# Memory squares in other buffers, later first loads of x, and another order for ACT in the second weight block of a two-layer encoder

## The chip, the cores and the metric

The kernel runs on one core of a Trainium2 chip, in one launch. The metric is the device time of one execution in microseconds (us). The engines are PE (TensorE, with PEld for its weight loads), DVE (VectorE), ACT (ScalarE), POOL (GpSimd) and SP (SyncE, which here only issues transfers). Transfers are issued by three queues: SP's and ACT's, and POOL's, which the profile names q1, q10 and q0.

## The reference

A two-layer encoder over 256 tokens `x` of width 2048, with 256 memory tokens `mem` of the same width. In each layer

```
h = rmsnorm(x) ; P = h @ w_in[l]            # 2048 x 7168, split among three mixers
A: short gated convolution (768 columns)
D: differential attention, 6 heads of 128 (two softmaxes of 64-wide halves, ALiBi)
M: cross-attention into the memory, 4 heads of 128:
   mkv = rmsnorm(mem, mem_norm_g[l]) @ w_mem_kv[l]      # 2048 x (512 keys + 512 values)
   mk  = rmsnorm(keys per head) * mem_k_norm_g[l]
x = x + concat(A, D, M) @ w_out[l]
```

All in float32. Only the memory part, `mem` to keys and values of both layers, and the loading of `x` are touched by the change.

## The kernel before, in words

**Products.** Every product is done in three matmuls of a reduced-precision format: an operand is split into a high half `hi` and a low half `lo`, and hi*hi, hi*lo and lo*hi are summed in a bank of PSUM (L312 to L314). `block` (L295) does one such product of 256 tokens with 512 columns of weights. It goes through the 16 row tiles of the weights in 8 chunks of two. For each chunk `load_w` (L274) has SP load 512 KB into `raw` (4 buffers), ACT makes `hi` from it (L290, scaled by the norm's gains; L286 without), DVE makes `lo` (L291, L287), each with 4 buffers, and PE does 12 matmuls of 128x512. So a chunk's weights can be made only when PE has done with the chunk four before, and loaded only when DVE has done with the one four before.

**Order of the work.** The program starts with four memory blocks: keys of layer 0, values of layer 0, keys of layer 1, values of layer 1 (the loop at L764). Then come the blocks of layer 0 on `x`, its output, and the same for layer 1. The `before` hook of `block` is called ahead of each chunk's load: `mem_piece` in the first block, `mem_norm` in the second, `x_load` in the third, `x_squares` in the fourth.

- `mem_piece` (L687) has SP load a piece of `mem` into `xs`, a tile that later holds x. PE turns it, a 128x128 tile at a time, into `pt` (L638, `rows_T`), and ACT and DVE split it into `memT` (L255, L256). In its calls for the sixth and the last chunk it calls `mem_squares` for the first two quarters.
- `mem_squares(c)` (L697) lets ACT square a quarter of the memory's columns, one instruction for each 128 tokens, to sum them into `ssm`. The squares themselves are written to a scratch tile of tag `nat` (3 buffers), where nobody reads them.
- After the first block ACT copies its two banks into `kraw` (L777). Then `mem_norm` (L704) calls `mem_squares(2)` ahead of the second block's first chunk and `mem_squares(3)` ahead of its second, starts `mem_slowly` (the norm's reciprocal root, spread out on DVE, then layer 0's keys) at its third, and loads small constants.
- `x_turned` (L642) brings a strip of x, 512 columns of all tokens, into a tile `xt` of tag `e` (2 buffers) with four transfers, POOL's in layer 0 (L648); five chunks later DVE transposes it (L652) and ACT and DVE split it into `xT`. Its four strips are put on the list at every second chunk of the second block; the first is due four chunks later, so that in the program's text it comes behind all the memory squares. Since the transfer needs nothing but a free buffer, the first two are issued at the program's start.
- `x_load` (L751) loads x a second time, in natural layout, into `xs` when PE has done with `mem`, and calls `rest_of_constants` (L142), a row of small DVE operations on the parameter vectors `vb` and `lam_in`.

**What sets the order on an engine.** The program's text, re-ordered by a scheduler that runs a timeline of its own; instructions marked `keep_in_program_order` keep their order among themselves on an engine. In the first two blocks all of ACT's and DVE's work on weights and `memT` is so marked (`in_order`, L245, `pinned`). Pieces of work that run beside the blocks are generators in `tasks`: `later(g, n)` (L200) makes one due n chunks on, and `run_side` (L217) runs what is due after each chunk. SP's queue is in order: a transfer that waits for its buffer holds back those behind it.

**Tags.** Tiles of one tag share its buffers in turn. `e` (2 buffers) holds the strips `xt` and later attention scores; `nat` (3) holds scratch, among it `lam_in`, squares and `th`; `ga` (1) holds `kraw`, then layer 1's key sheet (L780), then a gate of layer 0; `mqT` (1) holds the query sheet of layer 0 and later other things.

Of the kernel before, what the change touches and what calls it, by code (L numbers as in the profile page):

```python
# [10 lines left out]
F32 = mybir.dt.float32  # L11
# [18 lines left out]
HALF = 64  # L30
MH = W_MEM // P
EPS = 1e-6
NB = 512
# [14 lines left out]
def encoder(ctx: ExitStack, tc: tile.TileContext, x, mem, norm_g, w_in, conv_w, conv_b,  # L48
            dq_g, dk_g, lq1, lk1, lq2, lk2, head_g, mem_norm_g, w_mem_kv, mq_g, mk_g, w_out, out):
    nc = tc.nc  # L50
    x, mem, out = x[0], mem[0], out[0]

    def pool(name, bufs, space=None):
        kw = {"space": space} if space is not None else {}
        return ctx.enter_context(tc.tile_pool(name=name, bufs=bufs, **kw))
# [5 lines left out]
    tmp = pool("tmp", 2)  # L61
# [8 lines left out]
    def nm(s):  # L70
        uid[0] += 1
        return f"{s}_{uid[0]}"
# [13 lines left out]
    lam_in = tmp.tile([P, 4, DEPTH * HALF], F32, tag="nat", name="lam_in", bufs=3)  # L86
# [45 lines left out]
    def g_mnorm(l, k):  # L132
        return cva[:, l * KT + k:l * KT + k + 1]

    cvb = const.tile([P, 64], F32, name="cvb")
    hgain = const.tile([P, DEPTH], F32, name="hgain")
    kgain = const.tile([P, DEPTH], F32, name="kgain")
    mgain = const.tile([P, DEPTH], F32, name="mgain")
    neglam = const.tile([P, DEPTH], F32, name="neglam")
    lam_init = [0.8 - 0.6 * math.exp(-0.3 * l) for l in range(DEPTH)]  # L140

    def rest_of_constants():  # L142
        pb = ps_t.tile([P, NB], F32, tag="t", name="pvb")
        nc.tensor.transpose(pb[:, 0:64], vb, ident[0:64, 0:64])
        nc.vector.tensor_copy(cvb, pb[:, 0:64])
        for l in range(DEPTH):
            nc.vector.tensor_scalar(hgain[:, l:l + 1], cvb[:, 52 + l:53 + l], 1.0 - lam_init[l], None, ALU.mult)
        nc.vector.scalar_tensor_tensor(kgain, cvb[:, 48:48 + DEPTH], HALF ** -0.5, cvb[:, 50:50 + DEPTH],
                                       ALU.mult, ALU.mult)
        nc.vector.tensor_tensor(mgain, cvb[:, 54:54 + DEPTH], cvb[:, 56:56 + DEPTH], ALU.mult)  # L150
        pr = tmp.tile([P, 2, DEPTH, HALF], F32, tag="nat", name="lampr", bufs=3)
        for j in range(2):
            nc.vector.tensor_tensor(pr[:, j].rearrange("p l d -> p (l d)"), lam_in[:, 2 * j], lam_in[:, 2 * j + 1], ALU.mult)
        dots = small.tile([P, 2, DEPTH], F32, tag="dots", name="dots", bufs=1)
        nc.vector.tensor_reduce(dots, pr, AX.X, ALU.add)
        nc.scalar.activation(dots, dots, AF.Exp)
        nc.vector.tensor_tensor(neglam, dots[:, 1], dots[:, 0], ALU.subtract)
        for l in range(DEPTH):
            nc.vector.tensor_scalar(neglam[:, l:l + 1], neglam[:, l:l + 1], -lam_init[l], None, ALU.add)

    slopes = [2.0 ** (-8.0 * (h + 1) / DH) for h in range(DH)]


    class Steps:

# [4 lines left out]
        def __getattr__(self, op):  # L170
            return lambda *a, **k: self.ops.append((op, a, k))
# [24 lines left out]
    side, tasks = deque(), []  # L196
# [3 lines left out]
    def later(g, n):  # L200
        due[id(g)] = chunk[0] + n
        return g
# [192 lines left out]
    def normed(acc, gs, st, home):  # L395
        return normed_steps(nc.vector, acc, gs, st, home)
# [300 lines left out]
    def mem_squares(c):  # L697

        for t in range(NT):
            sq = tmp.tile([P, NB], F32, tag="nat", name=nm("sq"), bufs=3)  # L700
            tc.keep_in_program_order(
                nc.scalar.activation(sq, xs[:, t, c * NB:(c + 1) * NB], AF.Square, accum_out=ssm[:, t, c:c + 1]))  # L702
# [33 lines left out]
    def keys(l, nat):  # L736


        d = dram.tile([NA, B, NA, W_MEM // P * NT * B], F32, name=nm("kd"))
        flat = nat.rearrange("p b j t c -> p b (j t c)")  # L740
        for a in range(NA):
            tc.keep_in_program_order(nc.gpsimd.dma_start(d[:, :, a].rearrange("b c r -> c b r"), flat[a * B:(a + 1) * B]))
        tc.keep_in_program_order(nc.gpsimd.dma_start(flat, d.rearrange("b c a r -> (b c) a r")))
        yield 8
        tc.keep_in_program_order(nc.vector.transpose(
            mkT[l].rearrange("p j (t a i) -> p (j t) a i", t=NT, a=NA),
            nat.rearrange("p a j t c -> p (j t) a c")))
        yield
        tc.keep_in_program_order(nc.scalar.activation(mkT[l], mkT[l], AF.Copy, scale=mgain[:, l:l + 1]))
# [13 lines left out]
    mkT, mv, stm, away, acc_v = [], [], [], [], []  # L763
    for l in range(DEPTH):  # L764
        if l == 0:
            xT = T_tile("xT")
        mkT.append(keep.tile([P, MH, SEQ], F32, tag=f"mkT{l}", name=f"mkT{l}"))

        mv.append(keep.tile([P, NT, W_MEM], F32, tag="mv" if l == 0 else "bgx", name=f"mv{l}"))
        gm = lambda k: g_mnorm(l, k)  # L770
        pinned[0] = l == 0
        acc_k = block(memT, w_mem_kv[l], [(0, NB)], ALLK, gain=gm, before=mem_piece if l == 0 else x_load)
        if l == 0:

            kraw = keep.tile([P, NT, NB], F32, tag="ga", name="kraw")
            for t in range(NT):
                nc.scalar.copy(kraw[:, t], acc_k[t])  # L777
            stm.append(keep.tile([P, 6, NT], F32, tag="stm", name="stm"))
        if l > 0:
            tasks.append(later(keys(l, normed(acc_k, P, stm[0], sheets("ga"))), 10))  # L780
        acc = block(memT, w_mem_kv[l], [(W_MEM, NB)], ALLK, gain=gm, before=mem_norm if l == 0 else x_squares)
        pinned[0] = False
        acc_v.append(acc)
        if l > 0:
            for t in range(NT):
                nc.scalar.activation(mv[l][:, t, :], acc[t], AF.Copy, scale=col(stm[0], R, t))
            away.append(dram.tile([P, NT, W_MEM], F32, name=nm("mvd")))
            nc.sync.dma_start(away[-1], mv[l])
    for l in range(DEPTH):
# [18 lines left out]
        for b in order:  # L808
# [27 lines left out]
        mqT = keep.tile([P, MH, SEQ], F32, tag="mqT", name=nm("mqT"))  # L836
# [147 lines left out]
```

## Time and profile before

| | us |
|---|---|
| time, median of 3 runs | 936.94 (936.02 to 937.57) |
| the profiled execution's own time | 937.88 |
| its span, first to last instruction | 935.3 |
| PE busy | 921.1 |
| DVE busy | 671.3 |
| ACT busy | 499.2 |
| POOL busy | 16.2 |

The mean granted clock of PE over the span is 0.996 of full speed. The profile is of one execution; its page and the views made from its trace give times in us from the span's start, `L286` is a line of the kernel, and `acc<-hi,memT` names what an instruction writes and reads, buffer numbers left out. "xT<-xf" is thus one of the instructions that make x's transposed halves. In a timeline row stand start, duration, engine, line, operation, tiles, shapes and count, and in brackets the idle time ahead of it on its engine with what ended it. Of transfers the profile shows the issue on an engine's queue (SPq), and the packets by queue. Some matmul records can be missing from a trace, a few per cent.

In the page's costliest groups the pattern of the whole run can be seen: a weight chunk costs ACT 1052 ns (L286, 128x1024) or two times 716 (L290, 128x512), DVE 1222 or two times 745 ns, and PE 12 matmuls of about 390 ns each by the record, which overlap.

### The profile page before, as it was taken

The page shows a single profiled execution, that of the slowest core. Times are in us where ns is not written, and L with a number is a line of the kernel's source. Part 1 is how long each engine was busy: PE and PEld are TensorE (multiplying, and loading weights), DVE is VectorE, ACT ScalarE, POOL GpSimd, SP SyncE. Part 2 cuts the span into 40 slices and gives each one's busy share as a digit, 9 for nine tenths or more (in the row PEclk, how much of TensorE's full clock was granted, in tenths as well). Part 3 has the DMA queues.
Part 4 walks back from the last instruction along what each step waited for, and adds up shares of the span by engine and source line. Part 5 has one row for each costly group of instructions (what it writes and reads, how often), then busy time and mean ns, then how long its engine had stood idle before and what let it go on. Part 6 is the DMA issues. An engine that isn't in the chain of part 4 may idle for free.

```text
span 935.3 us, 12301 instructions
## 1 busy us (share of the span) xinstructions
PE 921.1 (98%) x4170; PEld 762.7 (82%) x4170; DVE 671.3 (72%) x1206; ACT 499.2 (53%) x779; POOL 16.2 (2%) x34
## 2 busy tenths in 40 slices
PE   6899999999999999999999999999999999999998
PEld 4688888888888888888888888888888888888886
DVE  3589977867789786566776757887898776558652
ACT  4666844576545554445555554568654454436431
POOL 2002100000000000000000000000000000000000
PEclk9999999999999999999999999999999999999999
DMA  9599778885678999989587766886889979988662
GB/s 249 172 297 267 247 266 230 244 237 171 195 211 219 240 269 248 237 271 248 205 256 263 243 198 201 235 246 185 241 226 222 257 215 252 250 243 235 215 216 78
DMA packets 251138, 215.05 MB, mean 230 GB/s; under 512 B 131182, under 2 KB 174020, under 8 KB 251076
## 3 DMA queue, kind: packets, MB, share of 16 engines
q1 hardware_dynamic: 248292, 208.76, 76.5%
q0 software_dynamic: 1440, 4.20, 1.8%
q10 hardware_dynamic: 1344, 1.33, 0.5%
q8 instruction: 32, 0.52, 0.2%
q14 instruction: 30, 0.25, 0.1%
HBM read 193.26 MB, written 20.97 MB: 229 GB/s over the span
## 4 chain that ended last, share of the span: by engine, by line
PE 98%; DMA 1%; ACT 0%; SPq 0%; issue 0%; DVE 0%; DVEq 0%
PE acc L313 31%; PE acc L312 31%; PE acc L314 31%; PE po L462 2%; DMA xs<-in_mem_dram 1%; PE s L615 1%; PE s L570 1%; PE s L569 1%; PE pt L638 0%; SPq L691 0%; ACT kraw L777 0%; SPq L280 0%; ACT sq L702 0%; ACT hi L290 0%; DVE xs L945 0%
## 5 line engine op out<-in xcount | busy, mean ns | idle before, releaser
L286 ACT CAST hi<-raw 128x1024 fp32r<-128x1024 f32 x288 | 302.8, 1052 | 349.7 <-PE acc L314 284.4
L287 DVE TENSOR_TENSOR lo<-raw,hi 128x1024 fp32r<-128x1024 f32 x288 | 351.7, 1222 | 188.3 <-ACT hi L286 184.9
L312 PE MATMUL acc<-hi,xT 128*128 128x512 f32 x896 | 350.5, 392 | 0.0
L314 PE MATMUL acc<-hi,xT 128*128 128x512 f32 x896 | 349.0, 390 | 0.0
L313 PE MATMUL acc<-lo,xT 128*128 128x512 f32 x896 | 348.9, 389 | 0.0
L314 PEld LDWEIGHTS acc<-hi,xT 128*128 128x128 f32 x896 | 168.2, 188 | 35.0
L313 PEld LDWEIGHTS acc<-lo,xT 128*128 128x128 f32 x896 | 168.3, 188 | 34.1
L312 PEld LDWEIGHTS acc<-hi,xT 128*128 128x128 f32 x896 | 168.2, 188 | 34.0
L312 PE MATMUL acc<-hi,yT 128*128 128x512 f32 x256 | 99.6, 389 | 0.0
L314 PE MATMUL acc<-hi,yT 128*128 128x512 f32 x256 | 99.6, 389 | 0.0
L313 PE MATMUL acc<-lo,yT 128*128 128x512 f32 x256 | 99.6, 389 | 0.0
L313 PEld LDWEIGHTS acc<-lo,yT 128*128 128x128 f32 x256 | 48.1, 188 | 10.1
L312 PEld LDWEIGHTS acc<-hi,yT 128*128 128x128 f32 x256 | 48.1, 188 | 10.1
L314 PEld LDWEIGHTS acc<-hi,yT 128*128 128x128 f32 x256 | 48.1, 188 | 9.8
L291 DVE SCALAR_TENSOR_TENSOR lo<-raw,cva,hi 128x512 fp32r<-128x512 f32 x64 | 45.8, 745 | 13.6 <-ACT hi L290 13.2
L290 ACT ACTIVATE hi<-raw,cva 128x512 fp32r<-128x512 f32 x64 | 42.6, 716 | 16.7 <-DMA raw<-in_w_mem_kv_dram 15.4
L313 PE MATMUL acc<-lo,memT 128*128 128x512 f32 x124 | 49.9, 403 | 0.0
L314 PE MATMUL acc<-hi,memT 128*128 128x512 f32 x124 | 49.3, 398 | 0.0
L312 PE MATMUL acc<-hi,memT 128*128 128x512 f32 x124 | 46.0, 404 | 2.5 <-ACT hi L290 2.5
L312 PEld LDWEIGHTS acc<-hi,memT 128*128 128x128 f32 x124 | 23.5, 194 | 7.8 <-ACT hi L290 3.0
L313 PEld LDWEIGHTS acc<-lo,memT 128*128 128x128 f32 x124 | 24.0, 193 | 6.0 <-DVE lo L291 0.9
L314 PEld LDWEIGHTS acc<-hi,memT 128*128 128x128 f32 x124 | 24.0, 194 | 4.9
(156 smaller groups left out, 643.0 us busy)
## 6 DMA issues: line engine op xcount, KB each, us to landing
raw<-in_w_in_dram SPq DMA_DIRECT2D x192, 512.0 KB, 4.4
raw<-in_w_out_dram SPq DMA_DIRECT2D x64, 512.0 KB, 4.1
raw<-in_w_in_dram SPq DMA_DIRECT2D x64, 256.0 KB, 4.3
raw<-in_w_mem_kv_dram SPq DMA_DIRECT2D x31, 512.0 KB, 6.2
d<-sh SPq DMA_DIRECT2D x80, 128.0 KB, 3.6
sh<-d SPq DMA_DIRECT2D x64, 128.0 KB, 4.5
d<-yn SPq DMA_DIRECT2D x40, 64.0 KB, 3.9
yn<-d SPq DMA_DIRECT2D x40, 64.0 KB, 4.4
```

Source lines behind the costliest of these rows:

```text
L286: nc.scalar.copy(hi, raw)
L287: nc.vector.tensor_tensor(lo_, raw, hi.bitcast(F32), ALU.subtract)
L290: in_order(nc.scalar.activation(hi[:, j], raw[:, j], AF.Copy, scale=gains_of(j)), nc.vector.scalar_tensor_tensor(lo_[:, j], raw[:, j], gai ...
L291: nc.vector.scalar_tensor_tensor(lo_[:, j], raw[:, j], gains_of(j), hi[:, j].bitcast(F32), ALU.mult, ALU.subtract))
L312: nc.tensor.matmul(acc[t], sh, hi, start=first, stop=False)
L313: nc.tensor.matmul(acc[t], sh, lo, start=False, stop=False)
L314: nc.tensor.matmul(acc[t], sl, hi, start=False, stop=last)
L462: nc.tensor.matmul(po[:, t, :], eT[:, i, t, k, :], v[:, k, h * P:(h + 1) * P], start=k == 0, stop=k == NT - 1)
L569: nc.tensor.matmul(s[c][:, i, :], qi, k_first(yT, c, h), start=True, stop=False)
L570: nc.tensor.matmul(s[c][:, i, :], qi, k_second(yT, k2, c, h), start=False, stop=True)
L615: nc.tensor.matmul(s[:, i, :], qT[:, h, i * P:(i + 1) * P], kT[:, h, :], start=True, stop=True)
```

## The change

Four things are done.

1. `mem_squares` writes its scratch to tag `e` instead of `nat`. The tag's two buffers are those of the strips of x, and all eight squares come ahead of the first strip in the program's text.
2. In the second block `mem_norm` calls `mem_squares(2)` ahead of the second chunk (k of 2) instead of the first, copies the first block's banks to `kraw` ahead of the third (k of 4) instead of right after the first block, calls `mem_squares(3)` ahead of the fourth (6 instead of 2), and starts `mem_slowly` at the fifth (8 instead of 4). The copies are now kept in program order.
3. The operations of `rest_of_constants` on DVE are kept in program order, by a wrapper `InOrder`.
4. Layer 1's key sheet takes tag `mqT` instead of `ga`.

In the built program the order on the queues and engines changes as follows. POOL issues the first eight transfers of strips behind a wait for ACT, four for each strip. ACT makes the second block's first weights right after the first block's last, then squares a quarter, makes the second weights, copies the two banks, makes the third, squares the last quarter, and goes on with weights. On PE the transposes of the fourth piece of mem (two row tiles each; the first piece is loaded in two parts) stand ahead of the first full chunk's matmuls, not among them. On SP the four loads of `lam_in` stand among the weights of the first block instead of behind four loads of the second. On DVE the first operations of `rest_of_constants` (L145 to L150) stand in the third block instead of the first, and `mem_slowly` runs two chunks later.

```diff
     def rest_of_constants():
+        vec = InOrder()
         pb = ps_t.tile([P, NB], F32, tag="t", name="pvb")
         nc.tensor.transpose(pb[:, 0:64], vb, ident[0:64, 0:64])
-        nc.vector.tensor_copy(cvb, pb[:, 0:64])
+        vec.tensor_copy(cvb, pb[:, 0:64])
...
+    class InOrder:
+
+
+        def __getattr__(self, op):
+            return lambda *a, **k: tc.keep_in_program_order(getattr(nc.vector, op)(*a, **k))
...
     def mem_squares(c):
 
         for t in range(NT):
-            sq = tmp.tile([P, NB], F32, tag="nat", name=nm("sq"), bufs=3)
+
+            sq = tmp.tile([P, NB], F32, tag="e", name=nm("msq"))
             tc.keep_in_program_order(
                 nc.scalar.activation(sq, xs[:, t, c * NB:(c + 1) * NB], AF.Square, accum_out=ssm[:, t, c:c + 1]))
 
     def mem_norm(k):
         load_constants({0: 1, 2: 2, 6: 0}.get(k))
-        if k == 0:
+        if k == 2:
             mem_squares(2)
-        if k == 2:
+        if k == 4:
+
+            for t in range(NT):
+                tc.keep_in_program_order(nc.scalar.copy(kraw[:, t], acc_k[t]))
+        if k == 6:
             mem_squares(3)
-        if k == 4:
+        if k == 8:
             tasks.append(later(mem_slowly(), 1))
...
         if l == 0:
-
             kraw = keep.tile([P, NT, NB], F32, tag="ga", name="kraw")
-            for t in range(NT):
-                nc.scalar.copy(kraw[:, t], acc_k[t])
             stm.append(keep.tile([P, 6, NT], F32, tag="stm", name="stm"))
         if l > 0:
-            tasks.append(later(keys(l, normed(acc_k, P, stm[0], sheets("ga"))), 10))
+            tasks.append(later(keys(l, normed(acc_k, P, stm[0], sheets("mqT"))), 10))
```

The other operations of `rest_of_constants` are changed like its first.

More of the change, by code (lines that the diff above doesn't have):

```diff
@@ L142, in rest_of_constants @@
     def rest_of_constants():
+        vec = InOrder()
         pb = ps_t.tile([P, NB], F32, tag="t", name="pvb")
         nc.tensor.transpose(pb[:, 0:64], vb, ident[0:64, 0:64])
[L145 removed]
+        vec.tensor_copy(cvb, pb[:, 0:64])
         for l in range(DEPTH):
[L147 to L150, printed above, removed]
+            vec.tensor_scalar(hgain[:, l:l + 1], cvb[:, 52 + l:53 + l], 1.0 - lam_init[l], None, ALU.mult)
+        vec.scalar_tensor_tensor(kgain, cvb[:, 48:48 + DEPTH], HALF ** -0.5, cvb[:, 50:50 + DEPTH],
+                                 ALU.mult, ALU.mult)
+        vec.tensor_tensor(mgain, cvb[:, 54:54 + DEPTH], cvb[:, 56:56 + DEPTH], ALU.mult)
         pr = tmp.tile([P, 2, DEPTH, HALF], F32, tag="nat", name="lampr", bufs=3)
         for j in range(2):
[L153 removed]
+            vec.tensor_tensor(pr[:, j].rearrange("p l d -> p (l d)"), lam_in[:, 2 * j], lam_in[:, 2 * j + 1],
+                              ALU.mult)
         dots = small.tile([P, 2, DEPTH], F32, tag="dots", name="dots", bufs=1)
[L155 removed]
+        vec.tensor_reduce(dots, pr, AX.X, ALU.add)
         nc.scalar.activation(dots, dots, AF.Exp)
[L157 removed]
+        vec.tensor_tensor(neglam, dots[:, 1], dots[:, 0], ALU.subtract)
         for l in range(DEPTH):
[L159 removed]
+            vec.tensor_scalar(neglam[:, l:l + 1], neglam[:, l:l + 1], -lam_init[l], None, ALU.add)
     slopes = [2.0 ** (-8.0 * (h + 1) / DH) for h in range(DH)]
+    class InOrder:
+        def __getattr__(self, op):
+            return lambda *a, **k: tc.keep_in_program_order(getattr(nc.vector, op)(*a, **k))
     class Steps:
```

## The prediction, made before the changed kernel was run

> **What bounds the kernel now.** I read the page first: how much of the span each engine is busy, and the chain that ended last.
>
> ```profile
> PE 921.1 (98%) x4170; PEld 762.7 (82%) x4170; DVE 671.3 (72%) x1206; ACT 499.2 (53%) x779; POOL 16.2 (2%) x34
> ...
> PE 98%; DMA 1%; ACT 0%; SPq 0%; issue 0%; DVE 0%; DVEq 0%
> ```
>
> PE is busy 921.1 of the span's 935.3 us and carries 98% of the chain. A gain is possible only where PE idles, about 14 us, or runs at half its clock. So the next view is PE in order of time through the first 115 us, where the change lies (start, us; in brackets the idle time before and what ended it).
>
> ```profile
> 10.67 0.61 PE L341 MATMUL acc<-lo,memT 128*128 128x512 f32 x2
> 16.30 1.04 PE L638 MATMUL pt<-ident,xs 128*128 128x128 f32 x4 [5.01 <-DMA xs<-in_mem_dram]
> ```
> ```profile
> 40.27 0.39 PE L314 MATMUL acc<-hi,memT 128*128 128x512 f32 x1
> 43.21 0.85 PE L312 MATMUL acc<-hi,memT 128*128 128x512 f32 x2 [2.55 <-ACT hi L290]
> ...
> 47.82 0.40 PE L312 MATMUL acc<-hi,memT 128*128 128x512 f32 x1
> ```
>
> Two stalls matter there, one in each fence: 5.01 us until a piece of mem has landed (16.30), and 2.55 us between the first and the second weight block, until ACT has made the second block's first weights (43.21). Behind each the clock is halved; the windows view (stretch, PE, PEld, DVE, ACT, POOL busy, granted clock, DMA share, GB/s) shows it, in stretches of 3.41 us:
>
> ```profile
> 9.54:12.95 3.41, 1.75 (x8) 1.12 (x6) 1.31 (x3) 1.70 (x3) 0.00 (x0) 1.00 1.07 214
> 12.95:16.36 3.41, 0.06 (x1) 0.09 (x2) 0.84 (x2) 0.00 (x1) 0.00 (x0) 1.00 1.04 280
> 16.36:19.78 3.42, 3.42 (x11) 2.85 (x12) 1.36 (x3) 1.92 (x4) 0.00 (x0) 0.50 1.08 364
> 40.26:43.67 3.41, 0.86 (x4) 0.30 (x2) 0.48 (x1) 3.41 (x9) 0.00 (x0) 1.00 0.33 124
> 43.67:47.08 3.41, 3.41 (x9) 2.49 (x8) 2.38 (x5) 3.41 (x9) 0.00 (x0) 0.50 0.54 109
> ```
>
> After a stretch with PE busy 0.06 or 0.86 us the clock is 0.50 for one stretch, after one with 1.75 us it stays 1.00. A half-speed stretch costs 3.42 / 2 = 1.7 us. What is saved here reaches the end, because PE is busy 731.4 of the later 735 us:
>
> ```profile
> 200.00:935.00 735.00, 731.37 (x3350) 609.84 (x3348) 524.17 (x918) 377.74 (x582) 0.00 (x0) 1.00 0.79 226
> ```
>
> **Step 1, x's first two strips leave the start.** Before, POOL issues their 8 transfers at once, and they take 8.9 us to land. In the changed build they follow the last memory squares on ACT.
>
> ```profile
> DMA to landing us min/median/max: 5.8/8.9/9.9
> ```
>
> The DMA view (queue, packets, MB, share of the 16 engines) over 4 to 14.5 us, then over 15 to 22 us, has POOL's queue as q0 and SP's, with mem and weights, as q1:
>
> ```profile
> q1 hardware_dynamic: 1049, 1.45, 60.0%
> q0 software_dynamic: 381, 1.04, 44.0%
> ```
> ```profile
> q1 hardware_dynamic: 2028, 2.53, 107.9%
> ```
>
> Alone, q1 moves 2.53 MB in 7 us, 361 GB/s; beside the strips it moved 1.45 MB in 10.5 us, which alone takes 4.0. So the strips cost q1 at most 6.5 us, and by their share of the engines at least 0.44 x 10.5 = 4.6. The changed build's PE order, however, puts two groups of transposes ahead of the first full chunk (a chunk is two row tiles: 0.5 MB of weights, 12 products), so PE now waits for the next piece of mem as well. Ahead of that piece's end lie 0.52 MB of weights and its own 0.26 MB: 2.2 us after 16.3, or 18.5 (before it was used here without a wait):
>
> ```profile
> 20.20 0.60 PE L638 MATMUL pt<-ident,xs 128*128 128x128 f32 x4
> ```
> ```profile
> 16.30:40.66 24.36, 24.36 (x109) 19.26 (x109) 13.79 (x29) 14.28 (x33) 0.00 (x0) 0.93 0.71 232
> ```
>
> PE would then resume at 12.0 to 13.9; I take the middle, 12.9. From its restart PE needed 24.36 us to the block's end, 0.6 of which is a transpose group that now lies earlier: 23.8 at the old clock, 22.1 without the half-speed stretch. Whether that stretch falls away is open: by the row of 9.54 a stretch now holds some 0.5 us of head and 0.6 of transposes, 1.1, between 0.86 (halved) and 1.75 (not). I count half of 1.7. The block ends at 12.9 + 22.95 = 35.85 instead of 40.66 (40.27 + 0.39): **4.8 us gained** (bounds: 12.0 + 22.1 gives 6.6; 13.9 + 23.8 gives 3.0). The weights keep pace: SP's chain of issues waits for the same landings, which all come earlier.
>
> **Step 2, ACT's order in the second block.** ACT's and one windows row:
>
> ```profile
> 36.54 1.34 ACT L290 ACTIVATE hi<-raw,cva 128x512 fp32r<-128x512 f32 x2
> 40.25 1.07 ACT L777 COPY kraw<-acc 128x512 f32<-128x512 f32 x2 [2.37 <-PE acc L314]
> 41.20 0.64 ACT L702 ACTIVATE sq<-xs 128x512 f32<-128x512 f32 x1
> ...
> 42.44 1.32 ACT L290 ACTIVATE hi<-raw,cva 128x512 fp32r<-128x512 f32 x2
> ```
> ```profile
> 34.00:36.00 2.00, 2.00 (x10) 1.36 (x9) 1.25 (x7) 0.00 (x0) 0.00 (x0) 1.00 0.00 0
> ```
>
> Now weights stand behind two bank copies (1.07) and two squares (1.2), which wait for the block's end. In the changed order the first weights follow those of 36.54 directly, then two squares, the second weights, and only then the copies. The DMA engines idle at 34 to 36, so the weights lie ready; the hi buffer is that of the first block's fifth chunk, long used. They are made by about 39.2, the low half 0.7 later, before PE needs them at 40.66. The copies delay the third chunk's weights to 3 us after the block's end; PE wants them after 5.4. No stall takes the place of the old one. From 40.66 to the second chunk at 47.82 PE spent 7.16 us on 12 products; a chunk at full clock takes 2.72 (seven from 47.82 to 66.89, below). **Gain 4.4 us**; 2.55 is its lower end, if the half clock came anyway.
>
> [...]
>
> **Step 3, what the strips cost where they land.** In the changed order both strips are issued from 3.4 us into the second block (after copies 1.07, weights 1.32 and a square 0.64, from 0.3 on). There they meet weights and x's reload. Rows before, and DMA over 66 to 74 us, when the third strip was in flight:
>
> ```profile
> 47.00:57.00 10.00, 10.00 (x45) 8.21 (x45) 8.80 (x27) 7.40 (x13) 0.00 (x0) 1.00 0.79 254
> 57.00:65.00 8.00, 8.00 (x37) 6.63 (x36) 5.51 (x7) 3.98 (x7) 0.49 (x1) 1.00 1.05 393
> ```
> ```profile
> q1 hardware_dynamic: 648, 1.26, 73.9%
> ```
> ```profile
> 42.57 0.35 SPq L104 DMA_DIRECT2D lam_in<-in_lambda_q_dram  x1
> ```
> ```profile
> 60.12 1.34 ACT L290 ACTIVATE hi<-raw,cva 128x512 fp32r<-128x512 f32 x2 [2.57 <-DMA raw<-in_w_mem_kv_dram]
> ```
> ```profile
> 66.89 0.39 PE L312 MATMUL acc<-hi,memT 128*128 128x512 f32 x1
> ```
>
> q1 alone moves 393 GB/s; beside a strip 1.26 MB in 8 us, alone 3.2 us: one strip costs 4.8, two 9.6. By the start's price two cost 6.5; I take this, since it too is two strips issued back to back. The DMA is free for 0.21 x 10 = 2.1 us of 47 to 57, and lambda's loads, issued from 42.57 on ahead of weights, move into the first block: I count 1. So the third block's first weights, which ACT awaited until 60.12, come 6.5 - 3.1 = 3.4 us later against PE (ends: 0, and 9.6 - 2.1 = 7.5). PE takes that chunk only at 66.89; but DVE has no such reserve:
>
> ```profile
> 60.88:108.10 47.22, 47.22 (x210) 39.06 (x209) 45.05 (x100) 34.61 (x69) 9.55 (x17) 1.00 0.89 258
> ```
> ```profile
> 34.76 0.23 DVE L145 COPY cvb<-pvb 128x64 f32<-128x64 f32 x1 [2.08 <-PE pvb L144]
> ...
> 60.88 1.42 DVE L291 SCALAR_TENSOR_TENSOR lo<-raw,cva,hi 128x512 fp32r<-128x512 f32 x2 [2.49 <-ACT hi L290]
> ...
> 104.45 0.74 DVE L291 SCALAR_TENSOR_TENSOR lo<-raw,cva,hi 128x512 fp32r<-128x512 f32 x1
> ```
> ```profile
> 105.43 0.40 PE L313 MATMUL acc<-lo,memT 128*128 128x512 f32 x1
> ```
>
> From that chunk's low half to the fourth block's last, DVE works 45.05 of 47.22 us, longer than PE's 16 x 2.72 = 43.5. Its lead over PE falls until a low half ends at 105.19 and is used at 105.43: 0.24 us. The lateness of 3.4 arrives there almost whole: PE stalls **3.2 us** (0 to 7.3). Nine small operations that move into this stretch of DVE (constants and a square root's last steps, none longer than the 0.23 of 34.76, so 2 us at most) fit into its 2.2 us of pauses; without these they are added.
>
> [...]
>
> The second layer's key sheet in another buffer waits for nothing on PE's path: the transpose that ends its use stands at the same place in DVE's order as before. I cost it at nothing.
>
> **Sum.** 4.8 + 4.4 - 3.2 = 6.0 us. The profiled execution took 937.88, so 931.9; it stands 0.94 above the median of 936.94, on whose scale that is **930.9 us**.
>
> **Rivals.** *The strips hide.* If the idle shares of 47 to 57 and the buffers ahead of ACT take them up, step 3 is 0: 9.2 us, 927.7. For it: the low half ended at 62.3 is used at 66.89, 4.6 us of lead. Against: DMA share 1.05 from 57 on.
> *The start gains little.* q1 may be slow there by itself; then PE waits for the second piece until 15 and pays the half clock: 40.66 - (15 + 23.8) = 1.9, in all 3.1 us, 933.8. Against: q0's 44% of the engines' time, and q1's pace once it is gone.
>
> *The strips starve the third and fourth block* and the kernel is slower. Place: the same queue, behind the strips; price: 9.6 us, the 2 us of small operations on top, and 1.7 of half clock if the stall comes in one piece: 13.3 against 9.2, 4.1 us lost, 941.0. It decides from a lateness of 9 us, that is when the strips' landing lasts to the third block's start. Against: the strips land in 8.9 us, and the third block begins 21.8 us after the second.
> [...]
> *The change does not take effect*: if ACT's first weights were late after all, step 2 is gone and 1.6 us remain, 935.3. The built order speaks against it.
>
> **How the numbers follow.** Forecast 0.45; hidden strips 0.21; weak start 0.15; clock 0.05; no effect 0.06; starved 0.08. A measurement of this kernel can tell about 0.2% (1.9 us) from no change: faster than 935.0 holds forecast, hidden, weak start and clock, 0.86; within, 0.07; slower, 0.07. The bounds together reach from 6.6 + 4.4 - 0 = 11.0 (925.9) to 3.0 + 2.55 - 7.3 = -1.7 (938.7), seldom all at one side; the range goes from 927.0, under the hidden case, to 935.5.
>
> **What would show it.** Step 1: PE's wait for mem ends at 12 to 14, q0 empty until 40. Step 2: no idle time and clock 1.00 where the blocks meet. Step 3: PE stalls on "ACT hi" or "DVE lo" in the third or fourth block, 3 us in all, with DVE nearly full. The forecast is wrong if PE waits for mem beyond 15, if the stalls there are absent, or exceed 7 us.

## The result, and the profile after

| | before | changed |
|---|---|---|
| time, median, us | 937.55 (6 runs, 936.02 to 938.02) | 929.18 (6 runs, 927.83 to 930.39) |
| ratio, 95% interval | | 0.9913 (0.9900 to 0.9925) |
| the profiled execution's time and span | 937.88, 935.3 | 927.83, 926.0 |
| granted clock, mean | 0.996 | 1.000 |

The changed kernel is 8.4 us faster; 930.9 was predicted. In a later set of runs, beside other kernels, it took 930.86 (6 runs, 930.00 to 931.62), 0.9932 (0.9920 to 0.9944) of the kernel before there, so 6.7 us faster. The profiled executions' spans differ by 9.3 us. The page's chain of work that ended last:

```profile
PE 90%; DVE 4%; ACT 2%; DMA 2%; issue 1%; DVEq 0%; SPq 0%; ACTq 0%
```

PE's share of it falls from 98% to 90%, since DVE, ACT and DMA now carry the chain at some places. Where did the 9.3 us come from? The first place is the start. PE in order of time:

```profile
10.65 0.63 PE L349 MATMUL acc<-lo,memT 128*128 128x512 f32 x2
11.12 1.04 PE L646 MATMUL pt<-ident,xs 128*128 128x128 f32 x8
11.91 0.70 PE L320 MATMUL acc<-hi,memT 128*128 128x512 f32 x2
```

The transposes that waited 5.01 us and began at 16.30 now stand right behind the head, with no idle time in brackets. The DMA view of 4 to 14.5 us has no q0 any more:

```profile
q1 hardware_dynamic: 2879, 3.69, 100.7%
```

q1 moved 3.69 MB there against 1.45 before. No stretch is at half clock (windows view, columns as before):

```profile
9.54:12.95 3.41, 3.41 (x21) 2.88 (x20) 2.46 (x5) 2.15 (x5) 0.00 (x0) 1.00 1.08 375
12.95:16.36 3.41, 3.41 (x19) 2.81 (x18) 2.33 (x6) 2.29 (x6) 0.00 (x0) 1.00 0.95 315
```

The second place is where the first two blocks meet. ACT:

```profile
26.84 1.34 ACT L298 ACTIVATE hi<-raw,cva 128x512 fp32r<-128x512 f32 x2 [1.32 <-DMA raw<-in_w_mem_kv_dram]
...
30.41 2.56 ACT L298 ACTIVATE hi<-raw,cva 128x512 fp32r<-128x512 f32 x4
...
34.10 1.33 ACT L298 ACTIVATE hi<-raw,cva 128x512 fp32r<-128x512 f32 x2
35.33 1.05 ACT L720 COPY kraw<-acc 128x512 f32<-128x512 f32 x2
...
52.96 1.34 ACT L298 ACTIVATE hi<-raw,cva 128x512 fp32r<-128x512 f32 x2 [4.14 <-DMA raw<-in_w_mem_kv_dram]
```

The four instructions of 30.41 make the first block's last weights and the second block's first; they end at 32.97, while PE is still at the first block's last chunk (from 31.19 on, below). The second chunk's weights follow two squares at 34.10, and only then the banks are copied, at 35.33, with no wait. The row of 52.96 is the other side of the change: the third block's first weights are awaited for 4.14 us.

To put a size on each step I compare when PE begins four chunks: the first block's last, the second block's second, the third block's first, the fourth block's last. Before (the other two rows, 47.82 and 66.89, are above):

```profile
37.51 0.39 PE L312 MATMUL acc<-hi,memT 128*128 128x512 f32 x1
...
107.75 0.39 PE L312 MATMUL acc<-hi,memT 128*128 128x512 f32 x1
```

The changed kernel, and behind it the waits of PE from 11 to 115 us (line, what ended the wait: us in all, times, longest):

```profile
31.19 0.73 PE L320 MATMUL acc<-hi,memT 128*128 128x512 f32 x2 [0.22 <-ACT hi L298]
...
37.09 0.61 PE L320 MATMUL acc<-hi,memT 128*128 128x512 f32 x2
...
56.13 0.39 PE L320 MATMUL acc<-hi,memT 128*128 128x512 f32 x1
...
64.97 0.50 PE L321 MATMUL acc<-lo,memT 128*128 128x512 f32 x1 [0.28 <-DVE lo L299]
...
98.11 0.39 PE L320 MATMUL acc<-hi,memT 128*128 128x512 f32 x1
```
```profile
PE acc L321 <- DVE lo L299: 0.5, 2, 0.3
PE acc L320 <- ACT hi L298: 0.2, 1, 0.2
```

| stretch, by PE's chunks | before | changed | second execution of the changed kernel |
|---|---|---|---|
| to the first block's last chunk | 37.51 | 31.19 | 31.59 |
| from there to the second block's second chunk | 10.31 | 5.90 | 5.92 |
| from there to the fourth block's last chunk | 59.93 | 61.02 | 64.15 |
| sum | 107.75 | 98.11 | 101.66 |

The first line is step 1: 6.3 us gained (4.8 predicted). The second is step 2: 4.4 (4.4). The third is step 3, where 22 chunks of 2.72 us take 59.84: 1.1 lost (3.2). 6.3 + 4.4 - 1.1 = 9.6, of which 9.3 are left at the end. The 1.1 are two waits for a low half, in the third block (0.28 us at 64.97) and in the fourth (0.27 at 92.76). The products next to each wait also start further apart than the usual 0.23 us, so that each wait delays PE by 0.53 us, twice what stands in the brackets. The second execution, profiled in the later set of runs (its own time 931.62, span 929.6), loses 4.2 us in the third line:

```profile
31.59 0.50 PE L320 MATMUL acc<-hi,memT 128*128 128x512 f32 x1 [0.24 <-ACT hi L298]
...
37.51 0.61 PE L320 MATMUL acc<-hi,memT 128*128 128x512 f32 x2
...
57.34 0.49 PE L320 MATMUL acc<-hi,memT 128*128 128x512 f32 x1 [0.63 <-ACT hi L298]
...
101.66 0.39 PE L320 MATMUL acc<-hi,memT 128*128 128x512 f32 x1
```
```profile
PE acc L321 <- DVE lo L299: 1.8, 4, 0.9
PE acc L320 <- ACT hi L298: 0.9, 2, 0.6
```

So the strips' price where they land is no constant. The windows view of 44 to 50 us, the changed kernel and then its second execution:

```profile
44.00:50.00 6.00, 6.00 (x28) 4.96 (x27) 3.82 (x13) 1.41 (x3) 0.00 (x0) 1.00 1.05 260
```
```profile
44.00:50.00 6.00, 6.00 (x29) 4.95 (x28) 2.66 (x9) 1.34 (x2) 0.00 (x0) 1.00 1.04 213
```

The DMA engines are full in both (1.05 and 1.04), but move 260 GB/s in one and 213 in the other. By queue, the strips' q0 moved 0.52 and 0.54 MB in these 6 us, and q1, with the weights, 1.04 and 0.74 MB. At the start (4 to 14.5 us) q1 moved the same in both, 3.69 and 3.68 MB. Why the engines moved less here is open; it is not known whether the two executions ran on the same chip. In the second execution ACT makes the third block's first weights at 56.56 instead of 52.96, and PE has to wait for them (its row of 57.34):

```profile
56.56 2.70 ACT L298 ACTIVATE hi<-raw,cva 128x512 fp32r<-128x512 f32 x4 [3.65 <-PE acc L321]
```

The brackets name PE, but the chunk that last used this buffer, four back, was done at 37.51 + 4 x 2.72 = 48.4; so it was the load that came late.

### The profile page after: what moved, and what is told of

Read it like the earlier page. It is cut to its first block, busy times and chain, and to the rows that moved or that the text cites. A ratio compares the mean times of both kernels' runs of the same rounds, so it can differ in the third digit from the quotient of the medians.

```text
span 926.0 us, 12301 instructions
## 1 busy us (share of the span) xinstructions
PE 919.4 (99%) x4170; PEld 761.5 (82%) x4170; DVE 670.7 (72%) x1206; ACT 498.6 (54%) x779; POOL 16.2 (2%) x34
## 4 chain that ended last, share of the span: by engine, by line
PE 90%; DVE 4%; ACT 2%; DMA 2%; issue 1%; DVEq 0%; SPq 0%; ACTq 0%
PE acc L321 29%; PE acc L322 29%; PE acc L320 29%; DVE lo L299 2%; PE po L470 2%; DMA raw<-in_w_mem_kv_dram 2%; ACT hi L298 1%; DVE xf L660 1%; PE s L623 1%; PE s L578 1%; PE s L577 1%; DMA xs<-in_mem_dram 0%; ACT msq L711 0%; DVE xT L267 0%; DVE memT L264 0%
## 5 line engine op out<-in xcount | busy, mean ns | idle before, releaser
L322 PE MATMUL acc<-hi,memT 128*128 128x512 f32 x124 | 48.4, 390 | 0.0
L320 PE MATMUL acc<-hi,memT 128*128 128x512 f32 x124 | 44.8, 395 | 0.2 <-ACT hi L298 0.2
```

Source lines behind the costliest of these rows:

```text
L320: nc.tensor.matmul(acc[t], sh, hi, start=first, stop=False)
L322: nc.tensor.matmul(acc[t], sl, hi, start=False, stop=last)
```

## The experiments

My theory after this comparison was the ledger: the three steps are separate, each with its own cause. Its rivals were the forecast's sizes, and that the gain needs both parts at once. Medians below stand beside the kernel before on the same chip.

**One part alone: the strips.** The kernel before with

```diff
-            sq = tmp.tile([P, NB], F32, tag="nat", name=nm("sq"), bufs=3)
+            sq = tmp.tile([P, NB], F32, tag="e", name=nm("msq"))
```

> The kernel before with one edit: the memory squares write to the strips' tag, so that the first two strips leave the start; ACT's order in the second block, the constants and the key sheet stay as before. Theory A, a ledger read from the two traces: PE's order aligned by instruction, the changed kernel is 6.1 us ahead at the end of the first block, 10.7 once the second block runs, and 9.4 after the fourth; so the start is worth 6.1, ACT's order 4.6, and the strips where they land cost 1.3, and that only because the second block has become 4.6 us shorter (DVE's lead over PE at the third block's first weights is 1.9 us there against 5.5 before). With the old gap still in the second block the lead is about 4.6 us larger, the landing costs nothing, and the gain is the 6.1 of the start alone: about 931.4 if the kernel before takes 937.5, ratio 0.9935. Theory B, the forecast's sizes: 4.8 gained and 3.2 lost, 1.6 us, about 935.9. Theory C, the gain is one thing and needs both parts: under 1 us.

Measured: 931.54 against 936.65, ratio 0.9952 (0.9939 to 0.9966). The 5.1 us gained are far more than the 1.6 of theory B and somewhat less than the 6.1 of theory A, whose ratio of 0.9935 lies just outside the interval. The parts are not as the ledger had them: by its trace (the shortest of five executions) the first block's last chunk begins at 30.32 (7.2 gained), and from the second block's second chunk to the fourth block's last pass 61.84 us (2.0 more than 22 chunks without a stall), so the landing costs something here too. Most of it is one wait of 0.72 us for a low half in the fourth block, and what follows it. The gap between the blocks is there as before, but in this execution with no half clock behind it (PE, then the windows):

```profile
36.02 0.73 PE L312 MATMUL acc<-hi,memT 128*128 128x512 f32 x2 [2.55 <-ACT hi L290]
...
39.51 0.73 PE L312 MATMUL acc<-hi,memT 128*128 128x512 f32 x2
```
```profile
33.40:36.84 3.44, 0.84 (x4) 0.33 (x3) 0.84 (x2) 3.44 (x9) 0.00 (x0) 1.00 0.28 108
36.84:40.25 3.41, 3.26 (x12) 2.06 (x12) 1.33 (x3) 3.41 (x9) 1.71 (x3) 1.00 0.46 153
```

From the first block's last chunk to the second block's second pass 9.19 us here instead of 10.31. The other four timed executions had a mean clock of 0.997 or 0.998, where one half-speed stretch is 3.41 / 2 / 929 = 0.0018; so each of them probably had one.

**One part alone: ACT's order.** The changed kernel with the squares in their old tag:

```diff
-            sq = tmp.tile([P, NB], F32, tag="e", name=nm("msq"))
+            sq = tmp.tile([P, NB], F32, tag="nat", name=nm("sq"), bufs=3)
```

> The changed kernel with one edit undone: the memory squares write to their old scratch tag, so that the strips are issued at the start again; ACT's new order in the second block stays. Theory A: the start is as slow as before, with PE's 5 us wait for mem and the half clock; the 2.55 us gap and the half clock where the first two blocks meet go: 4.6 us gained, less at most 1 that the third and fourth block give back since PE comes there earlier: 933 to 934 against 937.5, ratio 0.995 to 0.996. Theory B, the forecast's size: 4.4 gained, 933.1; it can't be told from A here. Theory C, the second block's weights are made in time only because the first block's start has become faster (their loads land earlier): the gap stays in part and the gain is under 2 us.

Measured: 931.75 against 936.65, ratio 0.9951 (0.9939 to 0.9964): 4.9 us. Rows of PE:

```profile
43.40 0.39 PE L320 MATMUL acc<-hi,memT 128*128 128x512 f32 x1
...
103.24 0.39 PE L320 MATMUL acc<-hi,memT 128*128 128x512 f32 x1
```

The second block's second chunk begins 4.4 us earlier than before (47.82), though the first block's last is 0.4 later (37.96): 5.44 us pass between the two instead of 10.31, 4.9 less. The 59.84 us to 103.24 are 22 chunks without any stall. So ACT's order is worth 4.4 to 4.9 by itself, the third and fourth block give nothing back without the strips, and the theory that both parts are needed falls.

**The strips earlier.** The changed kernel, the strips behind the fourth square instead of the eighth:

```diff
-            sq = tmp.tile([P, NB], F32, tag="e", name=nm("msq"))
+            sq = (tmp.tile([P, NB], F32, tag="e", name=nm("msq")) if c < 2 else
+                  tmp.tile([P, NB], F32, tag="nat", name=nm("sq"), bufs=3))
```

> The changed kernel with one edit: only the first four memory squares (of the first block) write to the strips' tag, the last four to the old scratch tag. The strips then wait for ACT's fourth square, which ended at 34.1 us in the changed kernel's trace, and not for the eighth at 38.5: they are issued 4.4 us earlier, into stretches of 34 to 40 us where the share of the DMA engines is 0.67 to 0.85. Theory A: the lateness of the third block's weights is what eats DVE's lead; the 1.3 us or so of idle transfer time that the strips now use shrink the lateness by as much, and of the 1.3 us that PE lost in the third and fourth block about 1 comes back: some 928.2 if the changed kernel takes 929.2. Theory B: PE's stalls there come from DVE's own work alone, whatever the transfers do: no difference, 929.2. Theory C: the strips now delay the second block's own weights, whose lead is 2 to 3 us: slower than 929.2, and PE waits on ACT's hi between 37 and 48 us.

Measured: 928.21 against 936.65, ratio 0.9907 (0.9894 to 0.9920). Its trace has no wait of PE in the third and fourth block, and the third block's first weights are made earlier than the 52.96 of the changed kernel (ACT, PE):

```profile
50.87 0.72 ACT L298 ACTIVATE hi<-raw,cva 128x512 fp32r<-128x512 f32 x1 [2.40 <-DMA raw<-in_w_mem_kv_dram]
```
```profile
55.71 0.39 PE L320 MATMUL acc<-hi,memT 128*128 128x512 f32 x1
...
96.51 0.39 PE L320 MATMUL acc<-hi,memT 128*128 128x512 f32 x1
```

From 55.71 to 96.51 are 40.80 us, fifteen chunks of 2.72 exactly; from the second block's second chunk (35.95) on 0.7 are lost, all in the second block. So lateness of transfers makes the stalls, not DVE's own work. By the times alone the gain over the changed kernel is not clear of noise: the interval overlaps that of 0.9913. One more thing is different in this build: the lambda loads stand behind the second block's first four loads again, as in the kernel before, and the chunk that the changed kernel makes at 26.84 after waiting 1.32 us for its load is not late; its first block's last chunk begins at 30.52, 0.7 earlier.

**The strips earliest.** The same with `if c == 0`, behind the second square:

> The changed kernel with one edit: only the first two memory squares write to the strips' tag, so that the strips are issued at about 28 to 30 us, in the first block, where the share of the DMA engines is between 0.2 and 0.8; with four squares they went at 34 us, and that kernel took 928.2 with no stall of PE from 13 us on. Theory A: with no stall left in the third and fourth block there is nothing more to gain by landing earlier: 928.2, within 0.5. Theory B: the last chunks of the first block are made 0.05 to 1.3 us before their use, and loads that share the DMA engines with strips come too late for them: PE waits on ACT's hi between 28 and 36 us and the kernel is 1 to 3 us slower than 928.2.

Measured: 926.13 against 937.25, ratio 0.9889 (0.9871 to 0.9906). The strips go out at 20.6 us, earlier than I had written. Neither theory has it: nothing was lost, and the median is 2 us below theory A's 928.2, though the interval overlaps that of the strips behind the fourth square. It was run once more beside the changed kernel:

> The kernel with the strips at 28 to 30 us once more, beside the changed kernel on one chip, as what the added loads are compared with and to see whether it beats the changed kernel. Theory A: 926.1, and 2 to 3 us below the changed kernel: 1.3 from the stalls of the third and fourth block, the rest from a block start that is not held up by 0.2 to 0.8 us of small waits in the first block. Theory B: its lead was an accident of one chip: within 1 us of the changed kernel.

> The changed kernel itself on the chip of the three others, as their common reference: 929.2, within 1, with PE's two stalls of 0.3 us in the third and fourth block again (theory A: they come from the order and the bytes, not from one execution); theory B: without them.

Measured: 927.44 (ratio 0.9898, 0.9883 to 0.9914) and, for the changed kernel, 930.86 (0.9932, 0.9920 to 0.9944), both against 937.54: 3.4 us better, and the intervals are apart, so its lead was no accident of one chip. The changed kernel itself missed my "929.2, within 1", and its trace has five stalls in the third and fourth block instead of two. In the second trace of the version with the earliest strips PE has no wait from 11 to 115 us. The second block's second chunk and the fourth's last, and ACT's one long wait before the first of them:

```profile
36.64 0.50 PE L320 MATMUL acc<-hi,memT 128*128 128x512 f32 x1
...
96.95 0.39 PE L320 MATMUL acc<-hi,memT 128*128 128x512 f32 x1
```
```profile
35.86 1.34 ACT L298 ACTIVATE hi<-raw,cva 128x512 fp32r<-128x512 f32 x2 [2.96 <-DMA raw<-in_w_mem_kv_dram]
```

60.31 us pass from one to the other, against 64.15 in the changed kernel: of the 5.0 us between the two spans (924.6 and 929.6) the landing is 3.8. ACT's wait of 2.96 at 35.86 is what is left of the strips' price, and PE hardly feels it. Another 0.9 us was there already at the second block's second chunk (36.64 against 37.51). The lambda loads are issued later in this version too, from 28.15 on instead of 18.31, and what they are worth without the strips was not measured. This version beats both kernels.

**One strip back at the start.** The changed kernel with `if (c, t) == (0, 0)` in the same place, so that the first strip finds a free buffer:

> The changed kernel with one edit: only the first memory square writes to the strips' tag, the others to the old scratch tag. So the first strip finds a free buffer and is issued at the program's start, the second waits for a square at about 28 us. Half the strips' bytes are thus back at the start. Theory A: what strips cost there goes by their bytes on the DMA engines, 6.5 us of delay for two and some 3 for one: PE waits 2 to 3 us for mem near 11 us, with a half clock behind it, and the start loses about half of its 6.1 us: 932 to 933.5, with no stalls in the third and fourth block, since the second strip lands early too (about 1 us back): 931.5 to 933. Theory B: one strip fits beside mem and weights before PE needs the piece (there is slack in the start), and costs nothing: 928 to 929. Theory C: the first small transfers from POOL cost the whole: 934 to 935.

Measured: 930.15 against 937.25, ratio 0.9936 (0.9919 to 0.9953). PE waits for mem again, in two smaller pieces:

```profile
13.30 0.63 PE L646 MATMUL pt<-ident,xs 128*128 128x128 f32 x4 [0.81 <-DMA xs<-in_mem_dram]
15.20 0.63 PE L646 MATMUL pt<-ident,xs 128*128 128x128 f32 x4 [1.27 <-DMA xs<-in_mem_dram]
...
34.39 0.62 PE L320 MATMUL acc<-hi,memT 128*128 128x512 f32 x2
...
39.83 0.39 PE L320 MATMUL acc<-hi,memT 128*128 128x512 f32 x1
...
99.67 0.62 PE L320 MATMUL acc<-hi,memT 128*128 128x512 f32 x2
```

The first block's last chunk begins at 34.39: 3.1 gained where the changed kernel gained 6.3. In this trace half the bytes cost half, as theory A had it. From 39.83 to 99.67 pass 59.84 us, no stall at all: of the 3.2 lost at the start the 1.1 to 4.2 of the landing come back, and the time stands between the changed kernel's 929.18 and 930.86, 1.4 us under theory A's range. That range counted a half clock behind the wait, which this trace does not have (mean clock 0.999); two of the six executions, at 0.996, took 931.95 and 932.23.

**The clock.** The kernel before with nine matmuls of zeros in the gap between the first two blocks:

```diff
         if k == 0:
+            warm_in_order(9)
             mem_squares(2)
```

> The kernel before with nine matmuls of zeros (128x512, nobody reads their result) on PE between the first and the second block, where PE idled for 2.55 us; nothing else is changed, the second block's first weights come as late as before. Theory A: the half clock of one 3.4 us stretch behind the gap comes from PE's idling, and PE's work in the gap keeps it away: the granted clock stays 1.00 there, the first chunk of the second block takes 2.7 to 2.9 us and not 4.6, and 1.7 us are gained (ratio 0.998). [...] Theory C: the added matmuls reach past the gap and delay the block: slower.

Measured: 935.62 against 937.25, ratio 0.9985 (0.9976 to 0.9994): 1.6 us. PE, then the windows:

```profile
41.19 2.12 PE L707 MATMUL warm<-zeros 128*128 128x512 bf16 x9
43.90 0.73 PE L312 MATMUL acc<-hi,memT 128*128 128x512 f32 x2 [0.59 <-ACT hi L290]
...
47.09 0.39 PE L312 MATMUL acc<-hi,memT 128*128 128x512 f32 x1
```
```profile
40.26:43.67 3.41, 3.05 (x14) 1.35 (x12) 0.00 (x0) 2.74 (x7) 0.00 (x0) 1.00 0.46 154
43.67:47.08 3.41, 3.13 (x12) 2.29 (x13) 2.17 (x4) 3.41 (x9) 0.00 (x0) 1.00 0.38 73
```

The weights come as late as before, but the chunk from 43.90 takes 3.19 us instead of 4.61, at clock 1.00. By itself this trace decides little: in the strips-alone trace the clock stayed at 1.00 behind the unfilled gap, and here the start has more half clock than before (0.75, 0.75, 0.50 and 0.75 in four stretches from 9.54 on), so that the trace's mean of 0.994 is the lowest of its twelve executions. Over all executions the mean granted clock is 0.9969 (12) against 0.9952 (23 of the kernel before): about one half-speed stretch less. So the idle time was the cause of the half clock, worth 1.4 us by the chunk's two times and 1.6 by the executions.

**The small parts.** Both undone (`vec = nc.vector` in `rest_of_constants`, `sheets("ga")` for the key sheet), then the first alone:

> The changed kernel with its two small parts undone: the constants' operations on DVE are free to be ordered by the scheduler again, and the second layer's key sheet is back in its old buffer. In the build, the lambda products leave the third block's stretch of DVE for the first block (five operations, some 1.2 us by their durations in the changed kernel's trace), the others stay near. Theory A: DVE has no pause left in the third and fourth block (0.35 us in 45.9), so what leaves it comes back in part: 0.5 to 1 us faster than 929.2, unless the operations in the first block delay a chunk there, where low halves are made 0.05 us ahead of their use. Theory B: both parts are worth nothing, within 0.3 us of 929.2.

> The changed kernel with the constants' operations on DVE free to be ordered by the scheduler again; the second layer's key sheet stays in its new buffer. With both small parts undone the kernel took 934.6 against 929.2, and its trace has DVE wait 5.68 us in the first block for the lambda loads, with the first lambda product in front of the splits of memT, and PE idle for 3.7 us behind that. Theory A: this product is placed there because nothing keeps it behind the weights, so that undoing this part alone gives the whole loss: about 934.5. Theory B: the key sheet's old buffer causes half or more of it (the keys' squares were early on ACT there): under 2 us of loss, 930 to 931.

Measured: 934.63 against 936.65, ratio 0.9983 (0.9973 to 0.9993), and 934.96 against 937.25, ratio 0.9975 (0.9965 to 0.9985). Undoing the constants' order alone takes back most of the gain, and undoing the key sheet as well adds nothing clear of the noise. My expectation for the pair, a small gain, was wrong. DVE and PE with the constants' order undone:

```profile
23.71 0.29 DVE L154 TENSOR_TENSOR lampr<-lam_in 128x128 f32<-128x128 f32 x1 [5.52 <-DMA lam_in<-in_lambda_k_dram]
```
```profile
24.44 0.52 PE L646 MATMUL pt<-ident,xs 128*128 128x128 f32 x3 [2.73 <-issue]
```

DVE waits 5.52 us for lambda in front of a split of memT, and PE behind it idles for 2.73. The lambda loads are issued from 18.31 on in the changed kernel, among the first block's weights; a product that needs them must not stand in the first block. In the kernel before and in the strips-alone build, neither of which has the wrapper, DVE does this product in the third block (68.21 and 63.72); so the wrapper is needed only beside the rest of the change.

**More to load.** The changed kernel, and the one with the earliest strips, with two loads that nobody reads:

```diff
+        if k in (12, 14):
+            tc.keep_in_program_order(nc.sync.dma_start(
+                mkT[0] if k == 12 else mv[0],
+                x[0:P, 0:1024].rearrange("p (k c) -> p k c", c=SEQ if k == 12 else W_MEM)))
```

> The changed kernel with two added loads of 0.52 MB each on SP's queue, ahead of the weights of the second block's last two chunks, into tiles that are written anew later (nobody reads what they bring); 1.05 MB at the 361 to 393 GB/s of that queue alone are 2.7 to 2.9 us in which the third block's weights can't be loaded. Theory A: the changed kernel has used up its reserve (DVE's low halves come 0.05 us before their use at three places, DVE pauses for 0.35 us in 45.9), so that 2 to 2.8 us reach PE as stalls in the third and fourth block, and the time is 931.2 to 932 if the changed kernel takes 929.2. Theory B: what is loaded there is hidden as most of the strips' lateness was: within 0.5 of 929.2.

> The same two added loads in the kernel that lets only the first two squares hold the strips back, which took 926.1 and whose DVE leads PE by 4.8 us at the third block's first weights and by 1.7 at the least place. Theory A: the same 2.7 to 2.9 us of lateness meet a reserve here; the lead of 1.7 and DVE's pauses take up most of them, and PE stalls for 0 to 1 us: 926.1 to 927. So the same load costs 2 us or more there and under 1 here. Theory B: what added loads cost does not hang on the lead: the same difference in both kernels.

Measured: 930.87 beside 930.86 without the loads, and 927.19 beside 927.44. By the times, 1.05 MB more cost nothing in either, and my expectation for the first is not borne out: the second expectation's theory B, the same cost in both kernels, is what the times fit. By the traces the third line of the ledger is 63.96 us with the loads in the changed kernel, 2.9 more than in its first execution and 0.2 less than in its second; with the earliest strips 60.64 instead of 60.31. The changed kernel differs by 3.1 us between its own executions there, so that one trace with the loads decides nothing. That the reserve was used up in it stays unproved by this pair; the second kernel's reserve did take the loads.

## Why the prediction came out as it did

**Step 1** was too small, 4.8 against 6.3, and each of its pieces was off. I took PE's restart at 12.9; it came at 11.12 with no wait at all, earlier than my lower bound of 12.0, which subtracted the strips' delay from an estimated landing at 18.5. The piece must have been there sooner; the delay itself fits: SP's load of `conv_w`, behind the pieces of mem, was issued at 16.24 before and at 10.46 now, 5.8 us earlier, within the 4.6 to 6.5. I counted half of the half-clock stretch; without an idle stretch there was none. Against these 1.8 + 0.85 us stand some 0.4, since both groups of transposes now follow the restart and not only one, and 0.5 for a chunk of the first block that came late (26.84, the wait of 1.32): from the second chunk to the last pass 19.28 us there and 18.79 with the strips behind the fourth square. About 0.2 is left over. The lambda loads, which I counted as relief for the second block, stand ahead of that chunk on the queue, and ACT waits for its load in both executions of the changed kernel (1.32 and 1.56 us) and in the strips-alone build (0.96, which PE doesn't feel), but not behind the same loads in the trace with more to load, nor where they are issued later. So they may be what delays it, and it isn't shown. The cause of step 1 itself is shown: the strips alone gained 7.2 there, with the strips left at the start nothing was gained there, and one strip back at the start gave half of it back.

**Step 2** was right, 4.4 for 4.4. Done alone it gave 4.9 on the same line of the ledger; the changed kernel's 5.90 hold 0.46 of small waits in that stretch. The half clock's share is 1.4 to 1.6 by the added matmuls (1.7 in my reckoning). But in the strips-alone trace the same 2.55 us of idling were followed by clock 1.00. So half clock behind such a gap is not certain in each execution. In the kernel before the stretches at 0.50 begin at 16.36 and 43.67, 8.00 x 3.41 us apart; in the trace with the constants' order undone one begins at 25.26, 2.6 x 3.41 us behind 16.36:

```profile
25.26:28.67 3.41, 3.41 (x10) 2.70 (x9) 1.88 (x8) 0.73 (x3) 0.00 (x0) 0.51 0.76 266
```

Why the gap has half clock behind it in the one execution and not in the other is not shown. The 0.05 that I gave under "clock" was for a gap that costs no clock; by the added matmuls the 2.55 us cost 1.4 to 1.6.

**Step 3** had the right mechanism and a size between two measured ones: 3.2 predicted, 1.1 and 4.2 in two executions. The lateness was well forecast: before, the third block's first low half began 6.0 us ahead of the block's first product (60.88 and 66.89), now 2.4 us (53.72 and 56.13), so 3.6 later against PE, for 3.4. "The lateness of 3.4 arrives there almost whole" is what failed in the first execution. DVE, its first row and its windows row to the fourth block's last low half:

```profile
53.72 0.75 DVE L299 SCALAR_TENSOR_TENSOR lo<-raw,cva,hi 128x512 fp32r<-128x512 f32 x1 [3.81 <-ACT hi L298]
```
```profile
53.72:99.71 45.99, 45.44 (x199) 36.65 (x198) 45.64 (x112) 36.25 (x72) 8.85 (x16) 1.00 0.88 268
```

DVE is busy 45.64 of 45.99 us (the forecast's stretch, up to the next block's first low half, which begins at 99.71). I had set aside its 2.2 us of pauses (47.22 less 45.05) for the small operations that move in, but a late DVE also pauses less: 0.35 us are left. Of the 3.6 us of lateness these 1.8, less 0.6 of added work (45.64 against 45.05), were made up on DVE, 1.1 became PE's two waits, and the rest, about 1.3, came out of the lead that DVE had at the stretch's end. In the second execution the weights came another 3.6 us later, and no reserve was left for that. For step 3 the rival *the strips hide* describes the first execution better than the forecast does, and the second not at all. That its total, 9.2 us, comes so near the first execution's 9.3 is luck: it has step 1 too small by 1.5 and step 3 at nothing.

**The edits at nothing.** The key sheet is worth nothing that the runs can tell, as costed; it was undone only together with the constants' order. The constants' order was costed only by what it moves into the third block; that it keeps a product which waits for lambda out of the first block was missed, and undoing it costs 4 to 6 us (0.9975 against 0.9932 and 0.9913). The forecast's sum was not touched by that, since the part was in the kernel.

For the profiled execution the forecast was 931.9 and 927.83 was measured: of these 4.1 us, 1.5 are step 1 and 2.1 step 3. In the second execution, 931.62, step 1 gave 1.1 more than forecast and step 3 cost 1.0 more: there the total came out right because two errors met. By the medians 8.4 and 6.7 us were gained, for 6.0.

## What to carry to other kernels

A transfer that nobody needs soon should not wait for "later" but for a named instruction at a place where the transfer engines idle (their share is 0.60 from 16.36 to 19.78 us and 0.52 from 19.78 to 23.20 in the changed kernel): by the traces the same two strips cost 6 to 7 us at the start, 1 to 4 us in the second block, and some 0.5 behind the second square. When a late producer has pauses and a lead of its own, subtract them from the lateness before adding the rest as a stall; and profile a second execution before believing the size of a stall that hangs on transfers. If a change pulls loads forward, look for the instructions that wait for them: what keeps those in order may be worth as much as the change.

## What the runs showed of the hardware

- At nearly the same share of the DMA engines (1.05 and 1.04, from 44 to 50 us) two executions of the changed kernel moved 260 and 213 GB/s; the stalls behind them differed by 3.1 us.
- The clock's toll differs as well: in 23 executions of the kernel before in one set of runs the mean granted clock was between 0.993 and 0.998, and the longest (939.38 us) was among those with 0.993, the shortest (934.45) among those with 0.998.
